# Second group of seven products of the last projection moved between the mixer's last tiles

## The chip, the cores and the metric

The kernel runs on one core of one Trainium2 chip. The metric is the device time of one execution in microseconds (us); lower is better. Engines: PE is TensorE, which multiplies; DVE is VectorE, ACT is ScalarE, POOL is GpSimd, SP is SyncE, which here only issues transfers (DMAs). PE writes its products into PSUM, which has eight banks of 128x512 fp32 here: four with the tag `mm` and four with the tag `sm`.

## The reference

One layer of a decoder: a token mixer in three branches, a gated merge, and a ConvFFN channel mixer, then a norm. SEQ is 512, D_MODEL 1024, D_FF 2816. The change touches only the last projection, `w_down`, and what runs beside it:

```python
def conv_ffn(u, w_up, conv_w, conv_b, w_down):
    h = causal_dwconv(u @ w_up, conv_w, conv_b)
    a, v = h[..., :D_FF], h[..., D_FF:]
    return (jax.nn.silu(a) * v) @ w_down
...
        x = x + conv_ffn(rmsnorm(x, ln2_g[i]), ffn_w_up[i], ffn_conv_w[i], ffn_conv_b[i], ffn_w_down[i])
    return rmsnorm(x, final_g)
```

## The kernel before

**Products in high and low halves.** Every fp32 factor is split into a high half (`wh`, `fh`: a cast on ACT, L195 for weights) and a low half (`wl`, `fl`: the difference from the high half, on DVE, L215 for weights). A product of two factors is three matmuls per 128 rows of the inner dimension: high by high, high by low, low by high, in this order (`mm3`, L234). So the low half of the weights is wanted only after two thirds of a tile's matmuls.

**Jobs.** The program is a list of jobs, run in order. A job has a block of weights, up to 1 MB, and a body of matmuls. Ahead of the body of job n stands `prepare`: DVE makes the low half of the weights of job n+1 (and a difference that hangs on it, `job.then`), a difference that forms the weights of job n+2 (`job.form`, L339) and then its cast on ACT in two halves, spread over the body's steps, and SP fetches the raw weights of job n+3. There are two buffers for raw weights, three for high halves and two for low halves. All engines but SP run their instructions in the order written. `step()`, called once behind each tile, emits what is due beside the matmuls: the second halves of casts, and one further piece of each running generator.

**Up projection (here: the mixer).** `up_jobs` yields 22 jobs, numbers 0 to 21; a pair of jobs, one for each half of `w_up`, makes two of the 22 row blocks k of the hidden state. Each job has two tiles of 24 matmuls into a `pu` bank. `up_evac` takes a tile out: one scaling on ACT (L1185), two passes of the convolution on DVE (L1188), Silu on ACT for the first half (L1190), a multiply on POOL for the second (L1193). A generator, `later`, then splits the result at a later step into `fh` (L1205) and `fl` (L1206), and for k below 16 makes the sums that the seven products need (`sums_of`).

**Down projection.** Row blocks 0 to 7 are the first group, 8 to 15 the second. In each group the product with `w_down` is computed by seven products of half-sized matrices instead of eight (a scheme of the Strassen-Winograd kind): `one` to `seven`, each a job of two tiles of 12 matmuls. They run into `sm` banks; `plus` (L1231) adds a bank to the tile of the residual, `X1[tb, h]`, on DVE. Several products add up in a bank X[i] or Z[i]: PE adds the next product into a bank from which DVE has read the last. `three`, `five`, `six`, `seven` and `four` have weights that are differences of quarters of the weight block; two quarters, W[0] and W[1], are kept in tiles named `w3`. Row blocks 16 to 21 are the plain ones: `blocks_of(h, ...)` multiplies them for the left and the right half of the output's columns, 72 matmuls each, and adds the banks to the residual (L1433). Behind the left half stands `norm_early`, behind the right one the final norm and the output.

The first group (`sevens_early`) runs between mixer jobs: W is loaded behind job 5, and one product stands behind each of the jobs 8 to 14 (`EARLY`). The second group runs behind the mixer, in `down()`, in this order: load of W (into the buffer of `uh2`, the mixer's own input), `two`, the first plain job of the left half, `one`, `five`, the second plain job, `six`, `seven`, `four`, `three`, the right half. `finish()` ahead of it runs all pending generators to their end.

**Tiles.** The pool `big` has 54 buffers of 128x512 (`T`). `ypool` has two buffers of four such tiles each (tag `xs`); they hold W of the first group, and after it eight tiles for the last row blocks (`spare`, the names `f4` and `s4`).

Of the kernel before, what the change touches and what calls it, by code (L numbers as in the profile page):

```python
# [10 lines left out]
F32 = mybir.dt.float32  # L11
# [5 lines left out]
P = 128  # L17
S = 512
# [65 lines left out]
def trunk(ctx: ExitStack, tc, out, x, rel_bias, ln1_g, w_in, b_gate, w_a, pool_w, pool_scale, w_b,  # L84
# [23 lines left out]
    def T(name, dt=F32, shape=(P, S)):  # L108
        return big.tile(list(shape), dt, name=name, tag="t")
# [4 lines left out]
    def SM(name):  # L114
        return psum.tile([P, S], F32, name=name, tag="sm")
# [204 lines left out]
    def sums_of(f0, f1, ah, al, found):  # L320


        sa, sb = T("sa"), T("sb")
        dve.tensor_tensor(sa[:, LO], f0[:, HI], f1[:, HI], OP.add)
        dve.tensor_tensor(sa[:, HI], sa[:, LO], f0[:, LO], OP.subtract)
        dve.tensor_tensor(sb[:, LO], f0[:, LO], f0[:, HI], OP.subtract)
        dve.tensor_tensor(sb[:, HI], f1[:, LO], sa[:, HI], OP.subtract)
        yield
        bh, bl = T("sbh", F32R), T("sbl", F32R)
        act.copy(ah, sa)  # L330
        act.copy(bh, sb)
        yield
        dve.tensor_sub(al, sa, ah.bitcast(F32))
        dve.tensor_sub(bl, sb, bh.bitcast(F32))
        for j, h, l, half in ((1, ah, al, LO), (2, ah, al, HI), (3, bh, bl, LO), (4, bh, bl, HI)):
            found(j, h[:, half], l[:, half])

    def diff(out, a, b):
        dve.tensor_tensor(out, a, b, OP.subtract)  # L339
        return out  # L340
# [816 lines left out]


    ACTS = {}
    spare = []  # L1160
    ff = {}

    def ff_cols():
# [19 lines left out]
    def up_evac(m, ps):  # L1183
        t = HC[m] = T("hc")
        act.activation(t, ps, AF.Identity, bias=ff["c1"][:, ff["b"] + m:ff["b"] + m + 1], scale=fw(2, m))  # L1185
        for k in range(2):
            sh = 2 - k
            dve.scalar_tensor_tensor(t[:, sh:], ps[:, :S - sh], fw(k, m), t[:, sh:], OP.mult, OP.add)  # L1188
        if m < KF:
            act.activation(t, t, AF.Silu)  # L1190
            return
        a = HC[m - KF]
        pool.tensor_tensor(a, a, t, OP.mult)  # L1193

        def later():
            yield
            k = m - KF
            if k in (KS, KS + 1):
                if k == KS:
                    spare.append(ypool.tile([P, 4, S], F32R, name="f4", tag="xs"))  # L1200
                h, l = (spare[-1][:, 2 * (k - KS) + i, :] for i in range(2))
            elif k >= KS or k % 2:
                h, l = T("fh", F32R), T("fl", F32R)
            if k >= KS or k % 2:
                act.copy(h, a)  # L1205
                dve.tensor_sub(l, a, h.bitcast(F32))  # L1206
                ACTS[k] = (h, l)
                if k < KS:
                    yield
                    p = k // 2  # L1210
                    if p == 6:
                        spare.append(ypool.tile([P, 4, S], F32R, name="s4", tag="xs"))
                    if p >= 6:
                        sums = [spare[0][:, 2 * (p - 6) + i, :] for i in range(2)]
                    else:
                        sums = [T("sah", F32R), T("sal", F32R)]
                    for _ in sums_of(HC[k - 1], a, *sums,
                                     lambda j, h, l: FS.__setitem__((j, p), (h, l))):
                        yield
                return  # L1220
            t = T("f0", F32R)
            act.copy(t[:, :256], a[:, :256])
            dve.tensor_sub(t[:, 256:], a[:, :256], t[:, :256].bitcast(F32))
            FS[0, k // 2] = (t[:, :256], t[:, 256:])

        running.append(later())
# [3 lines left out]
    def plus(tb, h, what):  # L1230
        dve.tensor_tensor(X1[tb, h], X1[tb, h], what, OP.add)  # L1231
# [38 lines left out]
    def side(j):  # L1270
        if j == "A11":
            return first_half
        if j in ("A12", "A22"):
            return lambda p, i: second_half(p, i + 2 * (j == "A22"))
        return lambda p, i: sums(j, p, i)

    def sevens_early():

        q, job = quarters(0)
        W, X, Z = [], {}, {}  # L1280

        def load():
            for h in range(2):
                W.append(ypool.tile([P, 4, S], F32, name="w3", tag="xs"))
                sp.dma_start(W[h], q(h, 1))

        def into(banks, name, adds, first):
            def use(i, product):
                if first:
                    banks[i] = SM(name)  # L1290
                product(banks[i], first, True, not first)
                for tb, h in adds(i):
                    plus(tb, h, banks[i])
            return use

        two = job(q(1, 0), side("A12"), into(Z, "p2", lambda i: [(i, 0)], True))
        one = job(q(0, 0), side("A11"), into(X, "p1", lambda i: [(i, 0)], True))
        one.then = lambda: diff(W[0], W[0], one.raw)
        five = job(None, side(1), into(Z, "p5", lambda i: [(2 + i, 1)], True), lambda: W[0])
        three = job(None, side(4), into(Z, "p3", lambda i: [(i, 1)], False), lambda: W[1])  # L1300
        three.then = lambda: diff(W[1], W[1], W[0])
        six = job(None, side(2), into(X, "p6", lambda i: [(i, 1)], False), lambda: W[1])
        seven = job(q(0, 0), side(3), into(X, "p7", lambda i: [(2 + i, 1)], False),
                    lambda: diff(seven.raw, W[1], seven.raw))
        four = job(q(1, 0), side("A22"), into(X, "p4", lambda i: [(2 + i, 0)], False),
                   lambda: diff(four.raw, four.raw, W[1]))
        return load, [two, one, five, three, six, seven, four]

    def down():

        q, job = quarters(1)
        W, X, Z, acc = {}, {}, {}, {0: {}, 1: {}}

        def load_w():
            both = upool.tile([P, KD, S], F32, name="w3", tag="uh")
            for at in range(2):
                W[at] = both[:, 4 * at:4 * at + 4, :]
                sp.dma_start(W[at], q(at, 1))

        def p2(i, product):  # L1320
            acc[0][i] = MM("pb")
            product(acc[0][i], True, False)

        def p1(i, product):
            X[i] = SM("p1")
            product(X[i])
            plus(i, 0, X[i])

        def p5(i, product):
            Z[i] = SM("p5")  # L1330
            product(Z[i])
            plus(2 + i, 1, Z[i])

        def p6(i, product):
            product(X[i], False, True, True)
            plus(i, 1, X[i])

        def p7(i, product):
            product(X[i], False, True, True)
            plus(2 + i, 1, X[i])  # L1340
            plus(2 + i, 0, X[i])

        def p4(i, product):
            product(acc[0][2 + i], False)
            plus(2 + i, 0, acc[0][2 + i])
            running.append(early(2 + i))

        def p3(i, product):
            acc[1][i] = Z[i]
            product(Z[i], False, False, True)  # L1350

        two = job(q(1, 0), side("A12"), p2)
        one = job(q(0, 0), side("A11"), p1)
        one.then = lambda: diff(W[0], W[0], one.raw)
        five = job(None, side(1), p5, lambda: W[0])
        six = job(None, side(2), p6, lambda: diff(W[1], W[1], W[0]))
        seven = job(q(0, 0), side(3), p7, lambda: diff(seven.raw, W[1], seven.raw))
        four = job(q(1, 0), side("A22"), p4, lambda: diff(four.raw, four.raw, W[1]))
        plain = blocks_of(0, acc[0], (0, 1), (2, 3))

        yield Call(load_w)
        yield two
        yield next(plain)
        yield one
        yield five
        yield from plain
        yield six
        yield seven
        yield four
        yield job(q(1, 1), side(4), p3)  # L1370
        yield from blocks_of(1, acc[1], (0, 1), ())

    def up_jobs():
        held = []
# [80 lines left out]
    def program():  # L1455
# [34 lines left out]
        for pair in range(2):  # L1490
            for h in range(2):
                yield from wo_jobs(pair, h)
            if pair == 0:
                yield Call(ff_cols)
        load, extra = sevens_early()
        for i, job in enumerate(up_jobs()):
            yield job
            if i == EARLY - 3:
                yield Call(load)
            if EARLY <= i < EARLY + 7:  # L1500
                yield extra[i - EARLY]
        yield Call(lambda: fin.setdefault("g", grow(final_g)))
        yield Call(finish)
        yield from down()

    jobs = list(program())
    weights = [j for j in jobs if isinstance(j, Job)]
# [181 lines left out]
MIX = "ZZ0zz1ggggaa"  # L1689
SSD_ORDER = ((0, 0, 1), (1, 0, 1), (0, 1, 1), (2, 0, 1), (1, 1, 1), (3, 0, 1), (2, 1, 1), (3, 1, 1))  # L1690
WARM = 19
EARLY = 8

# [1 line left out]
_INS = ['x', 'rel_bias', 'ln1_g', 'w_in', 'b_gate', 'w_a', 'pool_w', 'pool_scale', 'w_b',  # L1695
# [26 lines left out]
```

## Time and profile before

| | |
|---|---|
| median of 3 runs | 1042.22 us (1041.94 to 1042.29) |
| the profiled execution's own time | 1042.0 us |
| its span, first to last instruction | 1040.2 us |
| mean granted TensorE clock | 0.997 |
| PE busy | 1027.1 us, 99% of the span |
| DVE, ACT, POOL busy | 674.3, 473.9, 149.6 us |

The profile is one execution on the chip. In a line of a timeline the columns are start, length (us), engine, line of the kernel, operation, out<-in by the program's names (numbers of buffers left out), sizes, count, and in brackets the engine's idle time just before with what ended it. `p` are banks of the seven products, `pu` of the mixer, `pb` of plain tiles in `mm` banks. A line of the windows has the stretch, its length, then for PE, PEld (the loads of weights into the array), DVE, ACT and POOL the busy time and the count, then the granted TensorE clock, the DMA share and GB/s. Neighbouring matmuls overlap, so the time of a group is read from start to start.

### The profile page before, as it was taken

How to read it: one execution, taken by the hardware profiler on the slowest of the kernel's cores; microseconds unless marked ns; L12 is line 12 of the kernel's file. 1: busy time of each engine (PE TensorE's matmuls, PEld its weight loads, DVE VectorE, ACT ScalarE, POOL GpSimd, SP SyncE). 2: the span in 40 equal slices, each digit the busy share in tenths (PEclk: the TensorE clock that was granted, in tenths of full speed). 3: DMA queues.
4: the chain of work that ended last, by engine and by line, in shares of the span. 5: the costliest groups of instructions: out<-in, count | busy, mean ns of one | idle time of the engine just before them, and what ended most of it. 6: DMA issues, size and time to landing. Idle time of an engine off the chain costs nothing.

```text
span 1040.2 us, 13090 instructions
## 1 busy us (share of the span) xinstructions
PE 1027.1 (99%) x5204; PEld 861.4 (83%) x5204; DVE 674.3 (65%) x905; ACT 473.9 (46%) x765; POOL 149.6 (14%) x125
## 2 busy tenths in 40 slices
PE   9999999999999999999999999999999999999987
PEld 9998878898888877888888888898888888888775
DVE  6553566684366658766768666767668677755675
ACT  6432544442564364558446234554444534444242
POOL 1770000000000005110162500002111100111020
PEclk9999999999999999999999999999999999999999
DMA  8344312126222444452244526542333133334332
GB/s 292 109 133 131 118 44 75 31 66 197 81 82 81 111 124 116 136 142 81 71 124 162 162 81 229 180 142 82 93 110 122 41 99 104 125 119 137 126 101 81
DMA packets 119068, 120.76 MB, mean 116 GB/s; under 512 B 5315, under 2 KB 101382, under 8 KB 119007
## 3 DMA queue, kind: packets, MB, share of 16 engines
q1 hardware_dynamic: 118415, 119.07, 36.2%
q8 instruction: 41, 0.67, 0.3%
q10 hardware_dynamic: 592, 0.86, 0.2%
q14 instruction: 20, 0.16, 0.0%
HBM read 116.12 MB, written 2.22 MB: 114 GB/s over the span
## 4 chain that ended last, share of the span: by engine, by line
PE 96%; DVE 2%; ACT 1%; issue 0%; ACTq 0%; DVEq 0%
PE pa L234 35%; PE pu L234 22%; PE pb L234 11%; PE pqk L234 9%; PE p L234 6%; PE pa L1573 2%; PE ps L670 1%; PE pu L1387 1%; PE ppw L234 1%; PE pt L698 1%; PE po L711 1%; PE py L996 1%; DVE wl L215 1%; PE pa L1530 1%; PE pyo L1003 1%; ACT wh L195 0%
## 5 line engine op out<-in xcount | busy, mean ns | idle before, releaser
L215 DVE TENSOR_TENSOR wl<-raw,wh 128x2048 fp32r<-128x2048 f32 (+3 forms) x95 | 216.7, 2284 | 44.1 <-ACT wh L195 39.0
L195 ACT CAST wh<-raw 128x1024 fp32r<-128x1024 f32 (+3 forms) x188 | 189.3, 1026 | 61.3 <-DVE raw L339 23.7
L1188 DVE SCALAR_TENSOR_TENSOR hc<-pu,fcol,hc 128x510 f32<-128x510 f32 x88 | 65.8, 748 | 58.2 <-ACT hc L1185 56.5
L234 PE MATMUL pa<-uh,wh 128*128 128x512 f32 x384 | 98.5, 398 | 0.0
L234 PE MATMUL pa<-ul,wh 128*128 128x512 f32 x384 | 94.9, 389 | 0.0
L234 PE MATMUL pa<-uh,wl 128*128 128x512 f32 x384 | 94.9, 389 | 0.0
L234 PEld LDWEIGHTS pa<-ul,wh 128*128 128x128 f32 x384 | 72.1, 188 | 15.2
L234 PEld LDWEIGHTS pa<-uh,wl 128*128 128x128 f32 x384 | 72.1, 188 | 15.0
L234 PE MATMUL pu<-uh,wl 128*128 128x512 f32 (+1 forms) x352 | 83.7, 380 | 0.0
L234 PE MATMUL pu<-ul,wh 128*128 128x512 f32 (+1 forms) x352 | 83.5, 379 | 0.0
L234 PE MATMUL pu<-uh,wh 128*128 128x512 f32 (+1 forms) x352 | 83.5, 379 | 0.0
L234 PEld LDWEIGHTS pa<-uh,wh 128*128 128x128 f32 x384 | 70.3, 188 | 14.7 <-issue 1.0
L234 PEld LDWEIGHTS pu<-uh,wl 128*128 128x128 f32 x352 | 64.1, 188 | 12.8 <-DVE wl L215 0.3
L234 PEld LDWEIGHTS pu<-ul,wh 128*128 128x128 f32 x352 | 64.2, 188 | 12.5
L234 PEld LDWEIGHTS pu<-uh,wh 128*128 128x128 f32 x352 | 64.1, 188 | 12.4
L1193 POOL TENSOR_TENSOR hc<-hc 128x512 f32<-128x512 f32 x22 | 30.4, 1383 | 262.6 <-DVE hc L1188 227.5
L1185 ACT ACTIVATE hc<-pu,fcol,fcol 128x512 f32<-128x512 f32 x40 | 31.2, 780 | 78.9 <-PE pu L234 78.6
L958 POOL TENSOR_TENSOR xd<-xc,dec 128x512 f32<-128x512 f32 x6 | 6.4, 1060 | 333.9 <-DVE xc L952 315.0
L1085 ACT ACTIVATE sg<-pa,col 128x512 f32<-128x512 f32 x24 | 16.5, 688 | 54.5 <-PE pa L234 47.8
L691 ACT ACTIVATE sb<-sb,both 128x128 f32<-128x128 f32 (+1 forms) x72 | 30.1, 418 | 23.6 <-DVE both L688 13.4
L234 PE MATMUL pqk<-uh,wh 128*128 128x512 f32 x144 | 36.9, 394 | 0.0
L234 PE MATMUL pqk<-ul,wh 128*128 128x512 f32 x144 | 36.3, 389 | 0.0
(366 smaller groups left out, 1803.2 us busy)
## 6 DMA issues: line engine op xcount, KB each, us to landing
raw<-in_w_in_dram SPq DMA_DIRECT2D x25, 1024.0 KB
raw<-in_ffn_w_up_dram SPq DMA_DIRECT2D x22, 1024.0 KB
raw<-in_ffn_w_down_dram SPq DMA_DIRECT2D x11, 1024.0 KB
raw<-in_w_in_dram SPq DMA_DIRECT2D x20, 512.0 KB
raw<-in_w_o_dram SPq DMA_DIRECT2D x8, 1024.0 KB
raw<-in_w_b_dram SPq DMA_DIRECT2D x4, 1024.0 KB
al<-ad SPq DMA_DIRECT2D x16, 256.0 KB
w<-in_ffn_w_down_dram SPq DMA_DIRECT2D x4, 1024.0 KB
```

Source lines behind the costliest of these rows:

```text
L195: act.copy(job.high[:, :, o], job.raw[:, :, o])
L215: (eng or dve).tensor_tensor(l[:, :, o], job.raw[:, :, o], h[:, :, o].bitcast(F32), OP.subtract)
L234: pe.matmul(ps, l, r, start=first and n == 0, stop=last and n == total - 1, skip_group_check=again)
L670: pe.matmul(pss[i][:, o:o + w * P], q[r, n * P:(n + 1) * P], k[r, kb * P:(kb + w) * P], start=True, stop=True)
L691: act.activation(sb[:, off:off + w * P], sb[:, off:off + w * P], AF.Exp, bias=nm[:, n, h:h + 1], accum_out=ls[:, n, h:h + 1])
L698: pe.transpose(pt[:, o:o + P], sb[:, o:o + P], eye)
L711: pe.matmul(po[DH * hh:DH * hh + DH, n * P:(n + 1) * P], V[g, kb + i][:, (2 * cc + hh) * DH:(2 * cc + hh + 1) * DH], probs[2 * cc + hh, mb ...
L1085: act.activation(s, ps, AF.Sigmoid, bias=col[:, o:o + 1])
L1185: act.activation(t, ps, AF.Identity, bias=ff["c1"][:, ff["b"] + m:ff["b"] + m + 1], scale=fw(2, m))
L1188: dve.scalar_tensor_tensor(t[:, sh:], ps[:, :S - sh], fw(k, m), t[:, sh:], OP.mult, OP.add)
L1193: pool.tensor_tensor(a, a, t, OP.mult)
L1573: pe.matmul(first[2 * n + j][:, lo:hi], a[:, k, j * P:(j + 1) * P], b[:, k, lo:hi], start=a is wh and b is uh and k == 0, stop=a is wl and ...
```

## The change

The second group is written by the same function as the first (`sevens_down(g, keep)`). Its W is loaded behind mixer job 17 into `ypool`. `two`, `one`, `five` and `six` stand behind the mixer jobs 18, 19, 20 and 21 (`LATE`). Behind the mixer follow `seven`, the first plain job of the left half, `four`, the second plain job, `three` and the right half. The plain tiles of the left half open banks of their own and close them; those of the right half for the first two row blocks of the output go on in the banks Z of `five` and `three`. The eight `spare` tiles are gone from `ypool`; their content goes into `T` tiles.

```diff
@@ in up_evac @@
             k = m - KF
-            if k in (KS, KS + 1):
-                if k == KS:
-                    spare.append(ypool.tile([P, 4, S], F32R, name="f4", tag="xs"))
-                h, l = (spare[-1][:, 2 * (k - KS) + i, :] for i in range(2))
-            elif k >= KS or k % 2:
+            if k >= KS or k % 2:
                 h, l = T("fh", F32R), T("fl", F32R)
-            if k >= KS or k % 2:
                 act.copy(h, a)
                 dve.tensor_sub(l, a, h.bitcast(F32))
                 ACTS[k] = (h, l)
                 if k < KS:
                     yield
-                    p = k // 2
-                    if p == 6:
-                        spare.append(ypool.tile([P, 4, S], F32R, name="s4", tag="xs"))
-                    if p >= 6:
-                        sums = [spare[0][:, 2 * (p - 6) + i, :] for i in range(2)]
-                    else:
-                        sums = [T("sah", F32R), T("sal", F32R)]
-                    for _ in sums_of(HC[k - 1], a, *sums,
-                                     lambda j, h, l: FS.__setitem__((j, p), (h, l))):
+                    for _ in sums_of(HC[k - 1], a, T("sah", F32R), T("sal", F32R),
+                                     lambda j, h, l: FS.__setitem__((j, k // 2), (h, l))):
                         yield
@@ the seven products @@
-    def sevens_early():
+    def into(banks, name, adds, first=False, close=True):
+        def use(i, product):
+            if first:
+                banks[i] = SM(name)
+            product(banks[i], first, close, not first)
+            for tb, h in adds(i):
+                plus(tb, h, banks[i])
+        return use
+
+    def sevens_down(g, keep=False):
-        q, job = quarters(0)
+        q, job = quarters(g)
         W, X, Z = [], {}, {}
         def load():
...
         two = job(q(1, 0), side("A12"), into(Z, "p2", lambda i: [(i, 0)], True))
         one = job(q(0, 0), side("A11"), into(X, "p1", lambda i: [(i, 0)], True))
         one.then = lambda: diff(W[0], W[0], one.raw)
         five = job(None, side(1), into(Z, "p5", lambda i: [(2 + i, 1)], True), lambda: W[0])
-        three = job(None, side(4), into(Z, "p3", lambda i: [(i, 1)], False), lambda: W[1])
-        three.then = lambda: diff(W[1], W[1], W[0])
-        six = job(None, side(2), into(X, "p6", lambda i: [(i, 1)], False), lambda: W[1])
-        seven = job(q(0, 0), side(3), into(X, "p7", lambda i: [(2 + i, 1)], False),
+        if keep:
+            three = job(q(1, 1), side(4), into(Z, "p3", lambda i: [], close=False))
+            six = job(None, side(2), into(X, "p6", lambda i: [(i, 1)]), lambda: diff(W[1], W[1], W[0]))
+        else:
+            three = job(None, side(4), into(Z, "p3", lambda i: [(i, 1)]), lambda: W[1])
+            three.then = lambda: diff(W[1], W[1], W[0])
+            six = job(None, side(2), into(X, "p6", lambda i: [(i, 1)]), lambda: W[1])
+        seven = job(q(0, 0), side(3), into(X, "p7", lambda i: [(2 + i, 1)]),
                     lambda: diff(seven.raw, W[1], seven.raw))
-        four = job(q(1, 0), side("A22"), into(X, "p4", lambda i: [(2 + i, 0)], False),
+        four = job(q(1, 0), side("A22"), into(X, "p4", lambda i: [(2 + i, 0)]),
                    lambda: diff(four.raw, four.raw, W[1]))
@@ behind the mixer @@
-    def down():
...
-        yield Call(load_w)
-        yield two
-        yield next(plain)
-        yield one
-        yield five
-        yield from plain
-        yield six
-        yield seven
-        yield four
-        yield job(q(1, 1), side(4), p3)
-        yield from blocks_of(1, acc[1], (0, 1), ())
+    def down(rest, opened):
+
+        plain = blocks_of(0, {}, (), ())
+        yield rest["seven"]
+        yield next(plain)
+        yield rest["four"]
+        yield from plain
+        yield rest["three"]
+        yield from blocks_of(1, opened, (0, 1), ())
@@ program @@
-        load, extra = sevens_early()
+        first, between, _ = sevens_down(0)
+        second_, last_, opened = sevens_down(1, keep=True)
+        extra = {EARLY + i: between[w] for i, w in enumerate(
+            ("two", "one", "five", "three", "six", "seven", "four"))}
+        extra.update({LATE + i: last_[w] for i, w in enumerate(("two", "one", "five", "six"))})
         for i, job in enumerate(up_jobs()):
             yield job
             if i == EARLY - 3:
-                yield Call(load)
-            if EARLY <= i < EARLY + 7:
-                yield extra[i - EARLY]
+                yield Call(first)
+            if i == LATE - 1:
+                yield Call(second_)
+            if i in extra:
+                yield extra[i]
         yield Call(lambda: fin.setdefault("g", grow(final_g)))
         yield Call(finish)
-        yield from down()
+        yield from down(last_, opened)
...
-EARLY = 8
+EARLY, LATE = 8, 18
```

More of the change, by code (lines that the diff above doesn't have):

```diff
@@ L1159, in trunk @@
     ACTS = {}
-    spare = []
     ff = {}
@@ L1285, in load @@
                 sp.dma_start(W[h], q(h, 1))
[L1287 to L1294, printed above, removed]
         two = job(q(1, 0), side("A12"), into(Z, "p2", lambda i: [(i, 0)], True))
@@ L1304, in sevens_early @@
+        seven = job(q(0, 0), side(3), into(X, "p7", lambda i: [(2 + i, 1)]),
                     lambda: diff(seven.raw, W[1], seven.raw))
-        four = job(q(1, 0), side("A22"), into(X, "p4", lambda i: [(2 + i, 0)], False),
+        four = job(q(1, 0), side("A22"), into(X, "p4", lambda i: [(2 + i, 0)]),
                    lambda: diff(four.raw, four.raw, W[1]))
-        return load, [two, one, five, three, six, seven, four]
-    def down():
[L1311 to L1359, printed above, removed]
-        yield Call(load_w)
-        yield two
@@ L1363, in down @@
+        return load, dict(two=two, one=one, five=five, three=three, six=six, seven=seven, four=four), Z
+    def down(rest, opened):
+        plain = blocks_of(0, {}, (), ())
+        yield rest["seven"]
         yield next(plain)
-        yield one
-        yield five
+        yield rest["four"]
         yield from plain
-        yield six
-        yield seven
-        yield four
-        yield job(q(1, 1), side(4), p3)
-        yield from blocks_of(1, acc[1], (0, 1), ())
+        yield rest["three"]
+        yield from blocks_of(1, opened, (0, 1), ())
```

## The prediction

> **What bounds the kernel now.** I read the page first, then who waited for whom, then the end of the span in the timeline of each engine. The page says that TensorE (PE) is the bound over the whole span:
>
> ```profile
> span 1040.2 us, 13090 instructions
> PE 1027.1 (99%) x5204; PEld 861.4 (83%) x5204; DVE 674.3 (65%) x905; ACT 473.9 (46%) x765; POOL 149.6 (14%) x125
> PE 96%; DVE 2%; ACT 1%; issue 0%; ACTq 0%; DVEq 0%
> ```
>
> The change alters no count of matmuls, so it can only win what PE loses near the jobs that it moves. The waits tell where PE loses (columns: total us, times, longest):
>
> ```profile
> PE p L234 <- DVE x L1231: 3.1, 1, 3.1
> PE pcb L927 <- ACT xcv L1015: 1.0, 1, 1.0
> PE pb L234 <- DVE wl L215: 0.5, 1, 0.5
> ```
>
> The first and the third lie behind the mixer's last tile, inside `down()`. PE's timeline there, from the first product behind the mixer to the last matmul:
>
> ```profile
> 956.61 1.07 PE L234 MATMUL pb<-wh,fh 128*128 128x512 f32 x4
> ...
> 963.41 0.61 PE L234 MATMUL pb<-wh,fl 128*128 128x512 f32 x2
> 964.55 0.73 PE L234 MATMUL pb<-wl,f 128*128 128x512 f32 x2 [0.53 <-DVE wl L215]
> 965.13 0.62 PE L234 MATMUL pb<-wl,fh 128*128 128x512 f32 x2
> ...
> 995.06 0.61 PE L234 MATMUL p<-wl,s 128*128 128x512 f32 x2
> 998.75 1.40 PE L234 MATMUL p<-wh,sbh 128*128 128x512 f32 x4 [3.08 <-DVE x L1231]
> 999.95 1.91 PE L234 MATMUL p<-wh,sbl 128*128 128x512 f32 x4
> 1001.65 1.68 PE L234 MATMUL p<-wl,sbh 128*128 128x512 f32 x4
> ...
> 1005.93 1.07 PE L234 MATMUL pb<-wh,fh 128*128 128x512 f32 x4
> ...
> 1032.68 0.61 PE L234 MATMUL pb<-wl,fh 128*128 128x512 f32 x2
> ```
>
> In the mixer the rate of PE is that of the chain, which has a product job and a mixer job as one unbroken run of matmuls:
>
> ```profile
> 842.32 5.44 PE p L234 x24
> 847.75 10.88 PE pu L234 x48
> ```
>
> That is 0.2267 us for a matmul. Behind the mixer stand seven product jobs of 24 and twice 72 plain matmuls, 312 in all, which need 70.73 us. From 956.61 to the last issue (1032.68 plus two matmuls, 1033.13) they took 76.52. So 5.79 us are lost, and start to start they divide so: at 963.41 two matmuls cover 1.14 and the next two 0.58 where 0.45 is due, together 0.81; from 995.06 to 998.75 there are 3.69 where 0.45 is due, 3.24; and the 24 matmuls from 998.75 to 1005.93 take 7.18 instead of 5.44, 1.74. The last piece is a slower clock, as the windows show (PEclk is the third column from the end):
>
> ```profile
> 372.50:376.00 3.50, 3.50 (x19) 3.05 (x20) 0.00 (x0) 3.50 (x7) 0.00 (x0) 1.00 1.02 340
> 960.00:965.00 5.00, 4.47 (x20) 3.41 (x19) 3.39 (x3) 2.52 (x3) 0.92 (x1) 1.00 0.80 310
> 965.00:970.00 5.00, 5.00 (x24) 4.12 (x23) 3.91 (x2) 0.98 (x2) 0.00 (x0) 1.00 0.32 105
> 995.00:998.60 3.60, 0.67 (x3) 0.21 (x2) 3.60 (x4) 0.48 (x1) 0.00 (x0) 1.00 0.45 100
> 998.60:1002.00 3.40, 3.25 (x9) 2.67 (x10) 2.46 (x3) 2.47 (x4) 0.00 (x0) 0.64 0.52 203
> 1002.00:1006.00 4.00, 4.00 (x17) 3.18 (x16) 1.72 (x3) 1.03 (x2) 0.00 (x0) 0.88 0.59 172
> 1006.00:1010.00 4.00, 4.00 (x19) 3.31 (x18) 3.87 (x4) 2.00 (x2) 0.00 (x0) 1.00 0.23 90
> ```
>
> After a gap of 3.08 the granted clock was 0.64, then 0.88, then full again; after gaps of 0.5 and 1.0 it stayed 1.00.
>
> **Why PE waits 3.24.** `seven` adds its product to the bank X[i] that `six` has just left, and must wait until VectorE (DVE) has added `six` from that bank to the residual. DVE's queue at that place:
>
> ```profile
> 993.51 2.29 DVE L215 TENSOR_TENSOR wl<-raw,wh 128x2048 fp32r<-128x2048 f32 x1
> 995.72 2.28 DVE L339 TENSOR_TENSOR raw<-raw,w 128x2048 f32<-128x2048 f32 x1
> 997.93 1.28 DVE L1231 TENSOR_TENSOR x<-x,p 128x512 f32<-128x512 f32 x2
> ```
>
> Ahead of the add stand a low half (`wl`) and the difference that forms the weights of `four`, which DVE takes at full length between two adjacent product jobs. PE goes on 0.82 after the first add begins.
>
> **The change, part by part.** The prices come from two places of the trace. The first is the work of all engines behind mixer job 19 (of 0 to 21), whose last tile ended as the next job began, at 934.85:
>
> ```profile
> 934.85 1.98 PE L234 MATMUL pu<-uh,wh 128*128 128x512 f32 x8
> 935.05 0.78 ACT L1185 ACTIVATE hc<-pu,fcol 128x512 f32<-128x512 f32 x1 [3.73 <-PE pu L234]
> 935.86 1.53 DVE L1188 SCALAR_TENSOR_TENSOR hc<-pu,fcol,hc 128x510 f32<-128x510 f32 x2 [3.81 <-ACT hc L1185]
> 936.66 0.62 ACT L1205 CAST fh<-hc 128x512 fp32r<-128x512 f32 x1
> 937.31 0.69 DVE L1206 TENSOR_TENSOR fl<-hc,fh 128x512 fp32r<-128x512 f32 x1
> 937.56 1.59 POOL L1193 TENSOR_TENSOR hc<-hc 128x512 f32<-128x512 f32 x1 [4.08 <-DVE hc L1188]
> 937.92 3.38 DVE L215 TENSOR_TENSOR wl<-raw,wh 128x2048 fp32r<-128x2048 f32 x1
> ```
>
> The second is a load and what waits for it:
>
> ```profile
> 1000.15 2.29 DVE L215 TENSOR_TENSOR wl<-raw,wh 128x2048 fp32r<-128x2048 f32 x1 [0.94 <-ACT wh L195]
> ...
> 1007.51 2.00 ACT L195 CAST wh<-raw 128x1024 fp32r<-128x1024 f32 x2 [4.48 <-DMA raw<-in_ffn_w_down_dram]
> ...
> 1009.54 0.68 DVE L1231 TENSOR_TENSOR x<-x,pb 128x512 f32<-128x512 f32 x1
> ```
>
> *Moved:* `two`, `one`, `five`, `six` of the second group go between the last four mixer jobs; their 96 matmuls (21.76 us) leave the end and lengthen the mixer. Net on PE nothing, if DVE and ACT keep up there. *Does DVE keep up?* A mixer job with the product behind it takes PE 16.33. DVE then has two low halves, one of them slow (2.29 and 3.38), at most one difference (2.28), four passes of the convolution (3.06), two `fl` (1.38), two adds (1.38): 13.8. The first group, which already runs in this pattern and has more DVE work (it forms the sums as well), left no gap:
>
> ```profile
> 850.00:900.00 50.00, 50.00 (x222) 41.13 (x221) 36.47 (x37) 21.04 (x28) 5.24 (x4) 1.00 0.41 132
> ```
>
> So I cost the four moved jobs at nothing; PE's own 16.33 hides them. *Plain tiles:* `plain` no longer opens its banks with `two` nor leaves them to `four`: DVE gets 20 adds behind the products instead of 18, two of 0.68 more, under PE. *Weights:* the quarters W[0], W[1] now go into `ypool` during mixer job 17, so no load waits for `uh2`. On SyncE's queue they stand behind the fetch for mixer job 19 and ahead of that for `one`. A load's price is in the second fence: the fetch was free to go when that `wl` had read its buffer (1002.44), and the cast could begin at 1007.51: 5.1 us for 1 MB. Three MB take 15.3. W[0] is first read behind two mixer jobs, one product and a low half, 10.88 + 10.88 + 5.44 + 2.29 = 29.5 after the issue. Hidden, with 14 to spare.
>
> *The first wait (0.81)* came since `finish()` put the last tile's `fl` ahead of the low half of the plain weights. Now `six` stands there, and the last `fl` goes behind its first add. Gone.
>
> *The pair six, seven* stays adjacent: this is what is late next. The difference for `four` is no longer ahead of `six`'s adds (`plain0`, which needs none, is next in the pipeline of weights). Ahead stand the `fl` of the tile before the last and the low half of `seven`. The same order stood in before behind mixer job 19, in the first fence. The low half took 3.38 instead of 2.29 beside POOL's multiply, and ended 6.45 after 934.85. An add queued behind it would begin at 6.37 (0.08 before its end, as at 995.72), and PE could go on 0.82 later, at 7.19. `six` has issued its 24 matmuls at 5.44. So PE waits 1.75. If POOL's multiply lost the turn instead, `wl` would take 2.29 and the wait would be 0.66. I take 1.75, the row with the same neighbours. The second half of `seven` needs the second add (behind one `fl` and one add, ended by 8.5); PE gets there at 7.19 + 2.72 = 9.9. No second wait.
>
> *Behind it:* `four`'s weights are fetched when `seven`'s low half ends (6.45), land at 11.6, difference to 13.9, cast to 15.9, low half to 18.2; `four` starts at 1.75 + 21.77 = 23.5. 5 us to spare, since `plain0` is between. The three jobs after it are spaced by plain tiles in the same way. The tail behind the last matmul keeps its order.
>
> *The clock.* A gap of 1.75 lies between the 1.0 that left the clock alone and the 3.08 that cost 1.74, so its price is 0 to 1.74. The slow matmuls went from about 999.4 to 1002.8, 3.4 us; the 3.4 before that were idle for 2.75, or 80%. A gap of 1.75 can fill at most half of such a stretch, so I take 0. The Trainium skill, page "TensorE: Matmul & The Clock Gate", section "HAM oscillation — how this bites in real kernels", has it that gaps longer than about 3.4 us cost the clock; by that rule the sum here is the same, but the gap of 3.08 should have been free too, and the trace says otherwise.
>
> **Sum.** The profiled execution took 1042.0 (span 1040.2 and 1.8 around it). 1042.0 − 5.79 + 1.75 = 1038.0. The median of the runs, 1042.22, is 0.2 above that execution: 1038.2.
>
> **Rivals.** *The low half wins against POOL* (wait 0.66): 1037.1. For it: at that place POOL's multiply and `fl` begin within 0.25 of each other. Against: the row above.
> *The clock falls after the 1.75 gap:* 1.74 more, 1039.9.
> *The whole wait stays:* if the difference for `seven` or the convolution of the tile before the last sits 1.5 later in DVE's queue than I count, the add is again 3.2 late and the clock falls with it; only the 0.81 is won: 1041.4. By my count DVE is done with that convolution just as the last tile's is due, so the margin is thin.
> *The change doesn't free PE but stalls it: slower.* Eight 128x512 tiles that lay in `ypool` now come from the pool of 54. I count at most 50 alive at once (behind mixer job 12: 8 of the residual, 24 of the first group, 14 of pairs 4 and 5, and 4 of the mixer), at a place where both kernels hold the same, and at most 48 later. If I am short by five, a copy on ACT waits for the product still being multiplied, the next tile's evacuation queues behind it, and once four banks are full PE stands. A wait of one pair (16.3) less the banks' cover of one job (10.88) is 5.4 a time; one such wait already turns the 4.0 won into 1.4 lost, two give 1042.2 − 4.0 + 10.9 = 1049. The trace shows no waits for buffers, and neither for nor against beyond my count.
>
> **Chances.** 1038.2: 0.45; 1037.1: 0.18; 1039.9: 0.15; 1041.4: 0.10; slower by buffers: 0.08; the rest, around no change: 0.04. The range from 1036.5 (the 5.79 gone and nothing come) to 1040.3 holds the first three. A measurement of this kernel can tell about 0.2%, 2.1 us, from no change. Faster by more: the first three cases less a part of the third, 0.75. Within: that part, the fourth and the rest, 0.15. Slower: 0.10.
>
> **What would show it.** Right: PE without a gap from mixer job 18 to `six`; one wait of `p` for `x` of L1231's kind, 0.7 to 2 long, at the start of `seven`, directly behind a low half of about 3.4; no wait of `pb` for `wl`; granted clock 1.00 to the last matmul; PE's loss behind the mixer down from 5.79 to about 1.75. Wrong in size: a wait near 3 and a clock of 0.6 behind it. Wrong in kind: PE waiting in the mixer's last jobs for ACT or DVE, whose own wait is for PE's reading of an old tile, or for W's DMA.

## The result and the profile after

The changed kernel takes 1037.96 us (median of 6 runs, 1037.86 to 1038.57) against 1042.22 before: a ratio of 0.9961, interval 0.9949 to 0.9974. The forecast was 1038.2. The profiled execution took 1038.0, 4.0 less than that of before. From the page of the changed kernel:

```profile
span 1036.2 us, 13090 instructions
PE 1024.7 (99%) x5204; PEld 859.7 (83%) x5204; DVE 676.2 (65%) x907; ACT 473.8 (46%) x765; POOL 149.6 (14%) x125
PE 96%; DVE 1%; ACT 1%; DMA 1%; issue 0%; ACTq 0%; DVEq 0%
```

The counts on PE, ACT and POOL are those of before; DVE has the two adds more. PE is busy 2.4 less though it issues the same matmuls; 1.74 of it is the slow ones. PE's waits in the changed kernel, with one left in the part at stake (L1218 is the line of `plus` here):

```profile
PE p L234 <- DVE x L1218: 1.7, 1, 1.7
PE pa L1473 <- DVE relb L523: 1.1, 1, 1.1
PE pcb L927 <- ACT xcv L1015: 1.0, 1, 1.0
```

The wait of `pb` for `wl` is gone. PE's timeline at the wait that stayed, from `six` (972.72) over `seven` (980.04) to the plain job and the last matmul:

```profile
972.72 1.07 PE L234 MATMUL p<-wh,sah 128*128 128x512 f32 x4
...
977.25 1.07 PE L234 MATMUL p<-wl,sah 128*128 128x512 f32 x4
980.04 1.17 PE L234 MATMUL p<-wh,sbh 128*128 128x512 f32 x4 [1.72 <-DVE x L1218]
...
985.60 1.07 PE L234 MATMUL pb<-wh,fh 128*128 128x512 f32 x4
...
1028.67 0.61 PE L234 MATMUL pb<-wl,fh 128*128 128x512 f32 x2
```

From 977.25 to 980.04 there are 2.79 where 0.91 is due, 1.88 lost; `seven` itself takes 5.56 instead of 5.44, 0.12. The 240 matmuls from 972.72 to the last issue (1029.13) need 54.41 and took 56.41. So PE loses 2.00 behind the mixer's last tile, where it lost 5.79. That is 3.8 of the 4.0 that the two profiled executions differ by; the other 0.2 was there before the changed part began (the mixer job that starts at 880.23 before starts at 880.03 after) and is within what runs of one kernel differ by. The windows across the wait show the clock untouched:

```profile
975.00:980.00 5.00, 3.32 (x15) 2.43 (x13) 4.96 (x5) 2.79 (x4) 1.71 (x1) 1.00 0.00 0
980.00:985.00 5.00, 4.96 (x22) 4.13 (x23) 3.80 (x4) 0.00 (x0) 0.00 (x0) 1.00 0.71 227
```

What DVE did in the wait (its timeline, then POOL's):

```profile
971.61 1.53 DVE L1187 SCALAR_TENSOR_TENSOR hc<-pu,fcol,hc 128x510 f32<-128x510 f32 x2
973.73 1.53 DVE L1187 SCALAR_TENSOR_TENSOR hc<-pu,fcol,hc 128x510 f32<-128x510 f32 x2 [0.59 <-ACT hc L1184]
975.30 0.69 DVE L1200 TENSOR_TENSOR fl<-hc,fh 128x512 fp32r<-128x512 f32 x1
975.91 3.38 DVE L215 TENSOR_TENSOR wl<-raw,wh 128x2048 fp32r<-128x2048 f32 x1
979.22 0.67 DVE L1218 TENSOR_TENSOR x<-x,p 128x512 f32<-128x512 f32 x1
```
```profile
973.31 1.30 POOL L1192 TENSOR_TENSOR hc<-hc 128x512 f32<-128x512 f32 x1 [28.92 <-DVE hc L1187]
975.44 1.71 POOL L1192 TENSOR_TENSOR hc<-hc 128x512 f32<-128x512 f32 x1 [0.82 <-ACT fh L1199]
```

DVE's order is the convolutions, the `fl` of the tile before the last, a low half of 3.38 beside POOL's multiply, then the add; PE goes on 0.82 after the add begins. No difference for `four` stands there any more.

### The profile page after: what moved, and what is told of

It reads as the page before. It is cut to its first block, busy times and chain, and to the rows that moved or that the text cites. A ratio compares the mean times of both kernels' runs of the same rounds, so it can differ in the third digit from the quotient of the medians.

```text
span 1036.2 us, 13090 instructions
## 1 busy us (share of the span) xinstructions
PE 1024.7 (99%) x5204; PEld 859.7 (83%) x5204; DVE 676.2 (65%) x907; ACT 473.8 (46%) x765; POOL 149.6 (14%) x125
## 4 chain that ended last, share of the span: by engine, by line
PE 96%; DVE 1%; ACT 1%; DMA 1%; issue 0%; ACTq 0%; DVEq 0%
PE pa L234 35%; PE pu L234 22%; PE pb L234 11%; PE pqk L234 9%; PE p L234 8%; PE pa L1516 2%; PE ps L670 1%; PE pu L1324 1%; PE ppw L234 1%; PE pt L698 1%; PE po L711 1%; PE py L996 1%; DMA xin<-in_x_dram 1%; PE pyo L1003 1%; PE pst L982 0%; PE pxs L950 0%
```

## The experiments

The theory: PE loses time because `seven` follows `six` in the bank X while DVE is late with the add of `six`, and, when the gap is long, because the clock falls behind it. The rivals: the gain comes from the places between the mixer's tiles, or from W's early load.

**One plain job between six and seven, nothing else.** In the kernel before:

```diff
-        yield from plain
         yield six
+        yield from plain
         yield seven
```

> The kernel before with one edit: the second plain job of the left half stands between six and seven. Nothing is moved into the mixer. Theory (PE waits because seven follows six in the bank X and DVE is late with the add): the wait of 3.24 start to start and the slow clock behind it, 1.74, go; the first wait of 0.81 stays: 1042.2 - 4.98 = 1037.2. Rival (the gain comes from standing between the mixer's tiles, where DVE and ACT have room): the wait moves to another job of the tail and the time stays within 1 us of 1042.2.

Measured 1037.26, ratio 0.9955 (0.9943 to 0.9968). Of the two waits of PE in this part only the first is left:

```profile
PE pb L234 <- DVE wl L215: 0.5, 1, 0.5
```

Two swapped lines win as much as the whole change. No product of the second group stands in the mixer here.

**The weights alone.** The kernel before, with W of the second group in `ypool` and the spare tiles as `T` tiles:

```diff
-            both = upool.tile([P, KD, S], F32, name="w3", tag="uh")
             for at in range(2):
-                W[at] = both[:, 4 * at:4 * at + 4, :]
+                W[at] = ypool.tile([P, 4, S], F32, name="w3", tag="xs")
                 sp.dma_start(W[at], q(at, 1))
...
+            if i == 17:
+                yield load_2
```

> The kernel before with the part on the weights alone: W of the second group goes into ypool as in the change (the eight spare tiles go into T tiles), the order of the jobs stays. Theory: W's load behind the mixer was hidden, nothing waited for it, so 1042.2 within 0.4, with the waits of 0.5 and 3.1 as before. Rival (the load of 2 MB at the mixer's end delays DVE's first difference and all behind it): the wait ahead of seven shrinks and the time falls by 1 to 4 us.

Measured 1042.16, ratio 1.0001 (0.9992 to 1.0011). Both waits stand where they stood, in PE's timeline:

```profile
964.64 1.20 PE L234 MATMUL pb<-wl,fh 128*128 128x512 f32 x4 [0.53 <-DVE wl L215]
998.84 1.41 PE L234 MATMUL p<-wh,sbh 128*128 128x512 f32 x4 [3.08 <-DVE x L1218]
```

By itself the early load is worth nothing that these runs can tell (the interval is 0.1% to either side), and the tiles from the pool of 54 cost nothing.

**The mixer's part kept, four next to seven again.** In the changed kernel:

```diff
         yield rest["seven"]
-        yield next(plain)
         yield rest["four"]
         yield from plain
```

> The changed kernel with one edit: four directly behind seven, the plain jobs after both. The four jobs stay in the mixer. Theory: the difference for four (2.28) is again in DVE's queue ahead of six's adds, behind a low half of 3.38; the wait at seven grows from 1.88 start to start to about 4.1, the clock falls as in the kernel before (1.74 or more): 1038.0 + 2.2 + 1.8 = 1042.0. Rival (the move into the mixer is the gain): 1038.0 to 1038.5.

Measured 1042.51, ratio 1.0005 (0.9996 to 1.0014): the whole gain is gone with the jobs still in the mixer. DVE, then PE, then a window behind the gap:

```profile
976.52 3.38 DVE L215 TENSOR_TENSOR wl<-raw,wh 128x2048 fp32r<-128x2048 f32 x1
979.82 2.28 DVE L339 TENSOR_TENSOR raw<-raw,w 128x2048 f32<-128x2048 f32 x1
982.02 0.67 DVE L1218 TENSOR_TENSOR x<-x,p 128x512 f32<-128x512 f32 x1
```
```profile
977.85 1.07 PE L234 MATMUL p<-wl,sah 128*128 128x512 f32 x4
982.84 1.67 PE L234 MATMUL p<-wh,sbh 128*128 128x512 f32 x4 [3.92 <-DVE x L1218]
...
989.98 1.07 PE L234 MATMUL p<-wh,fh 128*128 128x512 f32 x4
```
```profile
983.00:986.00 3.00, 3.00 (x8) 2.30 (x8) 2.22 (x3) 2.58 (x4) 0.00 (x0) 0.55 0.50 193
```

DVE has the low half, the difference and the add in this order, as expected. PE lost 4.08 start to start, then 1.70 in `seven`'s 24 matmuls (7.14 instead of 5.44) at a clock of 0.55.

**The last wait taken away by order.** The changed kernel, with other work between the users of X:

```diff
-        yield rest["seven"]
         yield next(plain)
+        yield rest["seven"]
+        yield rest["three"]
         yield rest["four"]
         yield from plain
-        yield rest["three"]
```

> The changed kernel with another order behind the mixer: first plain job, seven, three, four, second plain job, right half. six and seven, and seven and four, no longer follow each other in the bank X. Theory: the last wait, 1.88 start to start, and the 0.1 of slower matmuls behind it go: 1036.0, no wait of p for x. Rival (DVE is simply behind at the mixer's end): PE waits for the low half of the plain weights or for a bank instead, and the time stays at 1038.

Measured 1036.42, ratio 0.9948 (0.9935 to 0.9960). The windows around the place of the old wait show PE full, though DVE is as busy as it was:

```profile
975.00:980.00 5.00, 5.00 (x24) 4.14 (x23) 5.00 (x4) 0.08 (x1) 1.59 (x1) 1.00 0.00 0
980.00:985.00 5.00, 5.00 (x24) 4.14 (x23) 3.91 (x5) 3.27 (x4) 0.00 (x0) 1.00 0.62 210
```

**Both waits taken away without the change.** The kernel before with the first edit of all, and `finish()` one job later:

```diff
         yield two
+        yield Call(finish)
         yield next(plain)
...
-        yield Call(finish)
         yield from down()
```

> The kernel before with two edits: the second plain job between six and seven, and finish() behind two instead of ahead of it. Nothing moves into the mixer, W stays in the buffer of uh2. Theory: finish() put the last tile's fl ahead of the plain weights' low half; without it the low half is done in time and the first wait of 0.81 goes as well, so all of the 5.79 is won without the change: 1036.4. Rival (the first wait is W's load or the end of the mixer as such): 1037.2 as with the first edit alone.

Measured 1036.51, ratio 0.9944 (0.9932 to 0.9957); PE has no wait left there. DVE takes the plain weights' low half ahead of the last `fl`, and its end at 963.28 comes in time for PE, which uses it from 964.07 (DVE, then PE):

```profile
959.90 3.38 DVE L215 TENSOR_TENSOR wl<-raw,wh 128x2048 fp32r<-128x2048 f32 x1
963.20 0.68 DVE L1206 TENSOR_TENSOR fl<-hc,fh 128x512 fp32r<-128x512 f32 x1
...
964.07 0.62 PE L234 MATMUL pb<-wl,f 128*128 128x512 f32 x2
```

So all of the 5.79 is to be had with the second group left behind the mixer.

**POOL out of the low half's way.** The changed kernel, with the last tile's multiply on DVE:

```diff
-        pool.tensor_tensor(a, a, t, OP.mult)
+        (dve if m == 2 * KF - 1 else pool).tensor_tensor(a, a, t, OP.mult)
```

> The changed kernel with one edit: the last tile's multiply on DVE (0.61 in its queue) instead of POOL. Theory (the low half of seven's weights stands still while POOL multiplies, 1.09 of its 3.38): the low half takes 2.29, the wait at seven falls from 1.88 start to start to about 1.4, the time by 0.5 to 1037.5. Rival (it is long for another reason, such as ACT's cast): it stays at 3.38 and the wait grows by 0.6 to 2.5.

Measured 1037.81, ratio 0.9957 (0.9944 to 0.9970). DVE and PE:

```profile
976.04 0.69 DVE L1192 TENSOR_TENSOR hc<-hc 128x512 f32<-128x512 f32 x1
976.65 0.68 DVE L1200 TENSOR_TENSOR fl<-hc,fh 128x512 fp32r<-128x512 f32 x1
977.25 2.28 DVE L215 TENSOR_TENSOR wl<-raw,wh 128x2048 fp32r<-128x2048 f32 x1
979.45 0.68 DVE L1218 TENSOR_TENSOR x<-x,p 128x512 f32<-128x512 f32 x1
```
```profile
980.28 1.16 PE L234 MATMUL p<-wh,sbh 128*128 128x512 f32 x4 [1.22 <-DVE x L1218]
```

The low half takes 2.28 and the wait shrinks from 1.72 to 1.22, as expected. The median of 1037.5 that was expected did not come: it moves by 0.15 only, less than the runs of one kernel differ by. In the profiled execution `six` began 0.74 later than in that of the changed kernel (973.46 against 972.72), which hides the gain. So the 0.5 is shown by the trace, not by the time.

**The add ahead of the low half, seven still behind six.** In the changed kernel `six` is marked late, and a late product job prepares the next jobs behind its first add:

```diff
+                    if i == 0 and j.late:
+                        j.prepare()
                     step()
...
+        six.late = keep
```

> The changed kernel with one edit: in six, what is prepared for later jobs (low half of seven, cast, fetch) is emitted behind the first add instead of ahead of it. The order on PE is as in the changed kernel, seven directly behind six. Theory (the wait is only the place of the add in DVE's queue): the add begins 3.2 behind the start of six, its end is before PE's 5.44, no wait: 1036.0. Rival (seven waits for its own weights): PE waits for the low half of seven instead, 1 to 2 us, and the time stays near 1038.

Measured 1036.54, ratio 0.9944 (0.9931 to 0.9957). DVE, then PE, which runs from `six` into `seven` (978.42) without a gap:

```profile
976.19 0.68 DVE L1218 TENSOR_TENSOR x<-x,p 128x512 f32<-128x512 f32 x1
976.78 2.79 DVE L215 TENSOR_TENSOR wl<-raw,wh 128x2048 fp32r<-128x2048 f32 x1
```
```profile
977.52 1.07 PE L234 MATMUL p<-wl,sah 128*128 128x512 f32 x4
978.42 1.07 PE L234 MATMUL p<-wh,sbh 128*128 128x512 f32 x4
```

So the wait came from the place of one add in DVE's queue; the weights of `seven`, the rival, hold nothing up.

**Two gaps between 1.7 and 3.1.** The changed kernel with an unread difference on DVE between the low half of `seven` and the add, of 128x512 (`:1`) and of 128x1024 (`:2`):

```diff
+        if keep:
+            seven.then = lambda: diff(W[0][:, :1], W[0][:, :1], W[1][:, :1])
```

> The changed kernel with one DVE operation more (a 128x512 difference that nobody reads, about 0.6) between the low half of seven and the add of six: the gap of PE grows from 1.72 to 2.3. For the clock, which stayed at 1.00 after 1.72 and fell after 3.08 and 3.92: if a stretch of 3.4 must be idle for four fifths, as it was ahead of the fall in the kernel before, 2.3 leaves it at 1.00 and the time is 1038.6; if half is enough, it falls for about 3.4 and the time is 1040.3.

> As the run with the gap of 2.3, the extra difference twice as long (128x1024, 1.2): the gap grows to 2.9. It can fill at most 85% of a stretch of 3.4, so whether the clock falls hangs on where the stretch begins; if it falls the time is 1040.9, if not 1039.2.

One run each: 1039.24 and 1041.29. PE and a window of the first, then of the second:

```profile
981.28 1.17 PE L234 MATMUL p<-wh,sbh 128*128 128x512 f32 x4 [2.32 <-DVE x L1218]
...
982.00:985.00 3.00, 3.00 (x14) 2.45 (x14) 2.54 (x2) 0.00 (x0) 0.00 (x0) 1.00 0.78 302
```
```profile
981.70 1.17 PE L234 MATMUL p<-wh,sbh 128*128 128x512 f32 x4 [2.86 <-DVE x L1218]
982.71 1.56 PE L234 MATMUL p<-wh,sbl 128*128 128x512 f32 x4
984.07 1.91 PE L234 MATMUL p<-wl,sbh 128*128 128x512 f32 x4
985.77 1.44 PE L234 MATMUL p<-wh,sbh 128*128 128x512 f32 x4
...
983.00:986.00 3.00, 3.00 (x9) 2.33 (x8) 2.91 (x2) 0.00 (x0) 0.00 (x0) 0.52 0.45 174
```

After 2.32 the clock stayed at 1.00; after 2.86 it fell, to 0.52 over this window. The times are 0.6 and 0.4 above the ones expected for these two cases; in both profiles `six` had begun 0.6 and 0.5 later than in the changed kernel, so that part arose ahead of the gap.

**The change and the better order on one chip.**

> The changed kernel itself, beside the next run on one chip: 1038.0, as measured.

> The changed kernel with the first plain job ahead of seven and three between seven and four, beside the changed kernel on one chip: by the theory 1.9 to 2.0 less than it, 1036.0 to 1036.4. Rival: the difference seen between the two calls was one of chips, and they agree within 0.5.

Measured 1038.35 (1037.61 to 1038.76) for the change and 1036.23 (1035.92 to 1037.01) for the other order: 2.1 apart, the 2.00 that PE still lost. A difference of chips, the rival, is thereby excluded.

## Why the prediction was right

**The bound and the terms.** The 5.79 that PE lost were the right account: each kernel with no wait left in this part came out at 1036.2 to 1036.5, where 1042.2 − 5.79 is 1036.4. The profiled execution took just the 1038.0 that the sum gave, and that is partly luck: PE lost 0.25 more at `seven` than the sum has, and 0.2 less was spent ahead of the changed part, which the sum doesn't have. The three pieces are separable: the first edit alone took away 3.24 and 1.74, the move of `finish()` the 0.81.

**The new wait.** The forecast was 1.75; measured are 1.88 and, in `seven` itself, 0.12 behind it, a term that the sum lacks. The row behind mixer job 19 gave the low half its 3.38, and that is what it took. It ended 6.57 after `six` began, not 6.45, since `fl` ahead of it began 2.58 after, not 2.46: the convolution of the tile before the last, for which I had called the margin thin, ended at 973.14 behind two long operations for the weights, POOL's multiply of that tile at 974.61, and ACT cast `fh` at 974.65 (its own cast of weights ran until 974.64, so the two came out together). That POOL's other multiply, the last tile's, is what makes the low half long is shown by the run with that multiply on DVE.

**The clock.** That a gap of 1.75 would leave it alone held, at 1.72. The reason I gave was that the stretch of 3.4 ahead of the fall had been idle for four fifths, and that a gap of 1.75 fills at most half of one. The run with 2.86 shows that four fifths are not needed: there the slow matmuls ran from about 983.1 to 986.5 (an estimate from the starts of the rows above), and of the 3.4 before that only 2.0 were idle, 59%. That is not far above the half, so the margin was smaller than I thought. Where the limit lies is not shown.

**The moved jobs.** They are free on PE, as forecast: there is no wait from the first of them to the end of `six`. A window over the first two of them:

```profile
900.00:950.00 50.00, 50.00 (x222) 41.43 (x221) 35.68 (x36) 22.14 (x29) 5.79 (x4) 1.00 0.34 112
```

But by themselves they are also worth nothing: with `four` put back next to `seven`, PE lost 4.08 and 1.70 there, as much as the 5.79 of before. The two steps that the prediction gave for the gain are the whole of it: the plain job between `seven` and `four`, which takes the difference for `four` out of the queue ahead of `six`'s add, and, for the 0.81, `six` in the place where `finish()` used to stand. Both can be had by order alone.

**The weights.** Their load was hidden, as forecast, but it did not stand where I said. The program does not hold SP to the order written, and SP issued the two loads in the first group's time, some 80 and 35 us ahead of mixer job 17, which begins at about 902 (SP's timeline):

```profile
821.60 0.37 SPq L1281 DMA_DIRECT2D w<-in_ffn_w_down_dram  x1
...
866.67 0.37 SPq L1281 DMA_DIRECT2D w<-in_ffn_w_down_dram  x1
```

My 29.5 and 15.3 were thus a bound that did not come into play.

**The rivals.** That the low half wins against POOL: no, it took 3.38. That the clock falls: not at 1.72. That the whole wait stays, because the convolution or the difference for `seven` sits 1.5 later in DVE's queue: no, the `fl` behind them began only 0.12 later than counted. A wait of that size came back by another cause, the difference for `four` put back ahead of the add (3.92 and a clock of 0.55); the plain job between is what keeps that away. That buffers stall the mixer: the run with the weights alone, which has the same eight tiles in the pool of 54, shows no wait.

## What to carry to other kernels

When PE waits for an add out of a bank, look at what stands ahead of that add in the other engine's queue before moving work: here one plain job in another place of PE's order won as much as the redesign, and an add put ahead of a low half in DVE's order took away the 2.00 that the redesign had left. Put a job that uses other banks between two jobs that share one, and emit the add that frees a bank ahead of preparations that are due later. A gap on PE can cost more than itself through the clock, so cut the long gaps first.

## What the runs showed of the hardware

In the profiles the slower clock came after gaps of 2.86, 3.08 and 3.92 and not after 1.72 or 2.32. Each time it cost about 1.7 (1.75, 1.74 and 1.70 in `seven`'s 24 matmuls), whatever the length of the gap. Read in finer stretches the granted clock is 0.50 for 3.4 each time: from 983.1 to 986.5 after 2.86, from 999.5 to 1002.9 in the kernel before, from 983.3 to 986.7 after 3.92. By the Trainium skill, page "TensorE: Matmul & The Clock Gate", section "HAM oscillation — how this bites in real kernels", only gaps above about 3.4 should have done so; two of the three were shorter, and the measurement decides. Whether 2.32 can make it fall when it lies otherwise in the stretch stays open, with one run at 2.32 and one at 2.86.

The fall may be missing in some executions. Of 41 runs of the kernel before that were timed beside these experiments, 36 have a mean granted clock of 0.995 to 0.997; the other five have 0.998 and took 1040.5 to 1040.9, about the 1.7 less that one fall costs. No run of a kernel whose waits in this part are 2.32 or shorter has a mean below 0.998. That the fall was absent in those five is not shown, since their profiles were not kept.

A low half on DVE that begins beside POOL's multiply takes 3.38 instead of 2.29 and is at its usual 2.28 when that multiply is not there. The excess follows the overlap: with the add put ahead, the low half begins later beside the same multiply and takes 2.79 (POOL's timeline in that run):

```profile
975.70 1.72 POOL L1192 TENSOR_TENSOR hc<-hc 128x512 f32<-128x512 f32 x1 [0.81 <-ACT fh L1199]
```

In both kernels the low half ends 2.14 to 2.15 after the multiply does, though it began 1.24 ahead of that end in one and 0.64 in the other. The Trainium skill, page "SBUF — State Buffer", section "SBUF: two separate sides", has one pair of ports that the two engines share, which a DVE operation with two inputs from SBUF needs too; whoever starts first holds it until its instruction ends. The trace agrees, with 1.1 of waiting against an overlap of 1.2 between 975.91 and the multiply's end at 977.15.
